# Two edges in the order of ScalarE and VectorE at the start of a gated recurrence

## The chip, the cores and the metric

The kernel runs on one core of one Trainium2 chip. The metric is the time of one execution on the device in microseconds, as the median of several runs; lower is better.

## The reference

One layer of a streaming encoder over 2048 tokens of width 1024, in float32. The input is normalised (RMSNorm) and projected by one matrix to eleven parts, which feed three groups of heads. Group A is a gated linear recurrence with 4 heads of 64x64 state, group B a mixer of trailing-window means, group C an attention with forgetting gates over 8 heads. Each output is gated, the three are concatenated and projected, normalised, and added to the input. The change touches group A:

```python
f_gate = lb + (1.0 - lb) * jax.nn.sigmoid(z)
log_f_a = jnp.log(jnp.maximum(f_gate, TINY))
k_a = (1.0 - lb) * jax.nn.sigmoid(-z)
...
# per chunk, state S: b = cumsum(log_f)
o = attn @ v + (q * exp(b)) @ S        # attn[t, s] = sum_d q[t] k[s] exp(b[t] - b[s]), s <= t
S = exp(b_last)[..., None] * S + (k * exp(b_last - b)).T @ v
```

## The kernel before, in words

The kernel first builds normalised, transposed halves of x (float16 high and low parts, `hTh` and `hTl`), tile by tile of 128 tokens. For each tile `x_parts` runs a square with a row sum on ScalarE (line 213), a scaling on VectorE (214), a power on GpSimd (217), a scaled copy on ScalarE (218), a subtraction on VectorE (220) and two transposing DMAs from SP's queue (221, 223).

The recurrence then goes through eight units `(g, ct)`: four groups of 512 tokens, and in each two halves of 128 channels (two heads). A unit has three parts.

- `hgrn_f` projects the gate input on TensorE (`pf`, 24 matmuls of 512 columns) and makes the features of the unit from it. ScalarE takes `pf` out of its bank (lines 254 and 255); then some twenty instructions of ScalarE, VectorE and GpSimd follow in a chain: `sg` (260), `E`, the running sum `b` (271), `nb` (274), the decayed keys `Kd`, `khat` (286, 287), `Qd`, `qhat` (289), and `el`, the decay of each of the four chunks (291).
- `hgrn_q` projects the queries (`pq`) and multiplies them into `Qd` and `qhat` (lines 301 to 309).
- `hgrn_unit` computes the outputs. Its part up to the first yield forms the nearest-neighbour products `pd` (327), masks them (329), transposes `khat` (`pk`, 333), and copies the result to `khT` on ScalarE (335). Then come six levels (64, 32, 16, 8, 4, 2), two between yields. A level forms differences of `b` on GpSimd (348, 349), their exponential `X` on ScalarE (350), `Z` = X times the queries in two halves on VectorE (355), the product `pl` on TensorE (359) and a masked copy into `at` on VectorE (363). After level 32 the state update takes `pu` = khT times the values (368) and eight updates of `S` on VectorE (378); after level 8 the state's share `po` of the output is formed (383). A last part adds `at` times the values (391), normalises and stores. X has four buffers, Z three.

The loop over the units runs the features of the next unit ahead of the levels of the current one. `fill` puts other projections in between: chunks of attention keys (`kq_chunk`) and token values of group A (`tok_i`). `feed` steps the x tiles from 8 on, one step a level.

The order in which instructions stand in the source isn't the order on an engine. A scheduler of the framework orders each engine's instructions before the program runs, from a cost model, with the order in the source as the priority among those that are ready. On the chip each engine then takes its instructions in that fixed order. `tc.issue_after(ins)` adds an edge to this ordering: every instruction traced in the block that runs on the engine of `ins` comes after `ins` there. It is no semaphore, and instructions of other engines in the block get no edge.

Of the kernel before, what the change touches and what calls it, by code (L numbers as in the profile page):

```python
# [15 lines left out]
AF = mybir.ActivationFunctionType  # L16
ALU = mybir.AluOpType
# [5 lines left out]
P = 128  # L23
# [31 lines left out]
def kernel(  # L55
# [138 lines left out]
            PE.matmul(ps, a[:, k, :], b[:, k, c0:c0 + n], start=i == 0, stop=i == 3 * KC - 1)  # L194


    last_pow = [None]

    xts = {}
    def x_dma(xpool, t, tag="xt"):  # L200
        xt = (xpool if tag == "xt" else ap).tile([P, D], F32, tag=tag, name=f"xt{t}", bufs=2)
        sp(nc.sync.dma_start(xt, xf[t * P:(t + 1) * P, :]))
        xts[t] = xt
# [21 lines left out]
    def x_load(xpool, t, tag="xt"):  # L225
        for _ in x_parts(xpool, t, tag):
            pass
# [20 lines left out]
    def hgrn_f(g, ct, wf, bank=None):  # L248
        u = f"_{g}_{ct}"
        pf = (bank or pj)(f"pf{u}")  # L250
        proj_cm(pf, wf, ct * P, g)
        yield
        z, E = tmp(f"z{u}"), tmp(f"E{u}")
        S.activation(E, pf, AF.Abs, bias=0.0, scale=INV)
        S.activation(z, pf, AF.Copy, bias=0.0, scale=INV)
        S.activation(E, E, AF.Exp, bias=0.0, scale=-1.0)
        S.activation(E, E, AF.Ln, bias=1.0, scale=1.0)
        sg = tmp(f"sg{u}")

        V.scalar_tensor_tensor(sg, z, 0.0, E, op0=ALU.min, op1=ALU.subtract)  # L260
        E1 = V if g == 0 else G
        E1.tensor_tensor(z, sg, z, op=ALU.subtract)
        lk = lbt[:, 8 + ct:9 + ct]

        V.tensor_scalar(E, sg, -43.0, None, op0=ALU.max)
        S.activation(E, E, AF.Exp, bias=0.0, scale=-1.0)
        S.activation(E, E, AF.Ln, bias=lbt[:, 4 + ct:5 + ct], scale=lbt[:, 2 + ct:3 + ct])
        V.tensor_tensor(E, E, sg, op=ALU.add)
        V.tensor_scalar(E, E, lbt[:, 6 + ct:7 + ct], None, op0=ALU.max)
        b = t512("b", f"b{u}")  # L270
        V.tensor_tensor_scan(b, d0, E, initial=0.0, op0=ALU.mult, op1=ALU.add)

        nb = t512("nb", f"nb{u}")
        V.scalar_tensor_tensor(nb, z, lk, b, op0=ALU.add, op1=ALU.subtract)

        lfo = sg
        E1.tensor_tensor(lfo.rearrange("p (n two) -> p n two", two=2),
                        E.rearrange("p (n two) -> p n two", two=2),
                        odd.unsqueeze(1).to_broadcast([P, GT // 2, 2]), op=ALU.mult)
        q_d, k_d = t512("Qd", f"Qd{u}"), t512("Kd", f"Kd{u}")  # L280
        E1.tensor_tensor(k_d, z, lfo, op=ALU.subtract)
        S.activation(k_d, k_d, AF.Exp, bias=lk, scale=1.0)
        S.activation(q_d, lfo, AF.Exp, bias=0.0, scale=1.0)
        kk = t512("khat", f"khat{u}")
        bt = b.rearrange("p (n t) -> p n t", t=P)
        G.tensor_tensor(kk.rearrange("p (n t) -> p n t", t=P), bt[:, :, P - 1:P].to_broadcast([P, 4, P]), nb.rearrange("p (n t) -> p n t", t=P), op=ALU.add)
        S.activation(kk, kk, AF.Exp, bias=0.0, scale=1.0)
        e = t512("qhat", f"qhat{u}")
        S.activation(e, b, AF.Exp, bias=0.0, scale=1.0)
        el = ap.tile([P, 4], F32, tag="el", name=f"el{u}", bufs=2)  # L290
        V.tensor_copy(el, e.rearrange("p (n t) -> p n t", t=P)[:, :, P - 1])
        feats[(g, ct)] = dict(nb=nb, b=b, qd=q_d, kd=k_d, kk=kk, qh=e, el=el)

    def hgrn_q(g, ct, wq):
# [17 lines left out]
    def run(steps):  # L312
        for _ in steps:
            pass

    def hgrn_unit(g, ct, va):
# [15 lines left out]
        for tt in range(4):  # L332
            PE.transpose(pk[:, tt * P:(tt + 1) * P], f["kk"][:, tt * P:(tt + 1) * P], idf)
        khT = t512("khT", f"khT{u}", 1)
        S.activation(khT, pk, AF.Copy, bias=0.0, scale=1.0)
        yield "B"

        for li, h in enumerate(LEVELS):
            X = t512("X", f"X{u}_{h}", 4)
            Z = Zs[zc[0] % NZ]  # L340
            zc[0] += 1
            bv = b.rearrange("p (n two h) -> p n two h", two=2, h=h)
            nbv = nb.rearrange("p (n two h) -> p n two h", two=2, h=h)
            Xv = X.rearrange("p (n two h) -> p n two h", two=2, h=h)
            n = GT // (2 * h)
            mid = bv[:, :, 0, h - 1:h].to_broadcast([P, n, h])
            E1 = G if h in POOL_LV else V
            E1.tensor_tensor(Xv[:, :, 1, :], bv[:, :, 1, :], mid, op=ALU.subtract)
            E1.tensor_tensor(Xv[:, :, 0, :], mid, nbv[:, :, 0, :], op=ALU.add)
            S.activation(X, X, AF.Exp, bias=0.0, scale=1.0)  # L350
            qv = qs.rearrange("p (t n two h) -> p t n two h", t=4, two=2, h=h)
            X5 = X.rearrange("p (t n two h) -> p t n two h", t=4, two=2, h=h)
            for hh in range(2):
                r = slice(64 * hh, 64 * hh + 64)
                V.tensor_tensor(Z[r, :, hh, :].rearrange("p t (n h) -> p t n h", h=h), X5[r, :, :, 1, :], qv[r, :, :, 1, :], op=ALU.mult)
            pl = pm(f"pl{u}_{h}")
            plv = pl.rearrange("p (t u c) -> p t u c", t=4, u=2)
            for tt in range(4):
                PE.matmul(plv[:, tt].rearrange("p u c -> p (u c)"), X[:, tt * P:(tt + 1) * P], Z[:, tt].rearrange("p u c -> p (u c)"),
                          start=tt == 0, stop=tt == 3, skip_group_check=True)  # L360
            n2 = 64 // h
            dst = at.rearrange("p t u (n two h) -> p (t u) n two h", two=2, h=h)[:, :, :, 1, :]
            V.copy_predicated(dst, masks[h].rearrange("p (n h) -> p n h", h=h).unsqueeze(1).to_broadcast([P, 8, n2, h]),
                              pl.rearrange("p (u n h) -> p u n h", u=8, h=h))
            if li == 1:
                pu = pm(f"pu{u}")
                for tt in range(4):
                    PE.matmul(pu[:, tt * P:(tt + 1) * P], khT[:, tt * P:(tt + 1) * P], va[:, tt, ct * P:(ct + 1) * P],
                              start=tt == 0, stop=tt == 3, skip_group_check=True)
                olds = []  # L370
                for tt in range(4):
                    old = Sst[ct][Scur[ct] % NS]
                    Scur[ct] += 1
                    new = Sst[ct][Scur[ct] % NS]
                    olds.append(old)
                    for hh in range(2):
                        r = slice(64 * hh, 64 * hh + 64)
                        V.scalar_tensor_tensor(new[r, r], old[r, r], f["el"][r, tt:tt + 1],
                                               pu[r, tt * P + 64 * hh:tt * P + 64 * hh + 64], op0=ALU.mult, op1=ALU.add)
            if li == 3:  # L380
                po = pm(f"po{u}")
                for tt in range(4):
                    PE.matmul(po[:, tt * P:(tt + 1) * P], f["qh"][:, tt * P:(tt + 1) * P], olds[tt], start=tt == 0, stop=False,
                              skip_group_check=True)
            next(xfeed, None)
            if li % 2 == 1:
                yield "L"
# [200 lines left out]

    run(hgrn_q(0, 0, wq))
    wk0 = load_w([(KCOL, 256)], "k0", pool=gwp)  # L590
    x_load(xpool, 6)
    x_dma(xpool, 8)
    x_load(xpool, 7)
    x_dma(xpool, 9)

    def feed():

# [14 lines left out]
    for n, (g, ct) in enumerate(units):  # L612
        nxt = units[n + 1] if n + 1 < len(units) else None

        def fill(j):
            if n == 0:
                if j % 2 == 0:
                    kq_chunk("k", 0, j // 2, g, wk0, kh_d, kl_d)
            elif n == 1:
                if j < 2:  # L620
                    tok_i(6 + j, wi, toks[1])
            elif ct == 0 and g + 1 < NG:
                t = 4 * (g + 1) + j
                if j == 0:
                    toks[g + 1] = new_tokens(g + 1)
                tok_i(t, wi, toks[g + 1])
            elif ct == 1:
                if j % 2 == 0:
                    kq_chunk("k", 0, j // 2, g, wk0, kh_d, kl_d)
            else:  # L630
                next(kq)
# [5 lines left out]
        if n == 0:  # L637
            fs, qs = hgrn_f(0, 1, wf, pm), hgrn_q(0, 1, wq)
            next(fs)
            next(qs)  # L640
            toks[1] = new_tokens(1)
            tok_i(4, wi, toks[1])
            tok_i(5, wi, toks[1])
            next(gen)
            next(gen)
            run(fs)
            run(qs)
            fill(0)
            next(gen)
            fill(1)  # L650
            fill(2)
            fill(3)
            next(gen)
            prev = gen
            continue
# [547 lines left out]
```

## Time and profile before

| | us |
|---|---|
| median of 3 runs | 1251.47 |
| lowest, highest | 1248.06, 1253.38 |
| the profiled execution | 1248.18 |
| its span, first to last instruction | 1246.4 |
| TensorE busy in the span | 1170.5 |
| VectorE busy | 812.2 |
| ScalarE busy | 609.5 |
| GpSimd busy | 403.7 |

In the profile PE is TensorE, PEld its weight loads, DVE VectorE, ACT ScalarE, POOL GpSimd and SPq the queue of SyncE that issues DMAs. Times in the rows are microseconds from the start of the span, and L with a number is a line of the kernel before. A row of a timeline gives start, time, engine, line, operation, output and inputs, shapes, count, and in brackets the idle time before it with what ended it. The eight units start, by their first product `pd`, at 60.38 us (0,0), 104.25 (0,1), 141.31 (1,0), 174.75 (1,1), 206.74 (2,0) and so on.

### The profile page before, as it was taken

Reading aid. Unit: us, or ns where it says so; the run is one execution under the profiler, and the core shown is the slowest. Engines: PE = TensorE matmul, PEld = TensorE weight load, DVE = VectorE, ACT = ScalarE, POOL = GpSimd, SP = SyncE. Lnnn points to the kernel's source line nnn. Section 1 sums busy time; section 2 is a strip of 40 time slices with the busy share of each in tenths; the row PEclk is TensorE's granted clock in tenths of the full one; section 3 lists DMA queues with packets and bytes.
Section 4 is the critical chain, followed back from the end, with each engine's and each line's share of the span. In section 5 each row is a group of like instructions: output and inputs, shape, how many; then the busy total and the mean of one; then the engine's idle time right before and its main releaser. Section 6 shows DMA issues by size and latency. Waiting matters only on the chain.

```text
span 1246.4 us, 25487 instructions
## 1 busy us (share of the span) xinstructions
PE 1170.5 (94%) x9949; PEld 749.9 (60%) x9949; DVE 812.2 (65%) x1736; ACT 609.5 (49%) x1176; POOL 403.7 (32%) x500
## 2 busy tenths in 40 slices
PE   5877999999999999999999999999989899999998
PEld 3445667655644588884447767755555555555544
DVE  5787878887433243214364799788788888888522
ACT  5756444553121222212122677667767676777611
POOL 2645555553130020002230223234334343434400
PEclk9988999999999999999999999999999999999999
DMA  9646100113175232101112343285223222321263
GB/s 226 184 115 170 44 17 18 52 35 93 43 183 142 71 107 71 35 2 43 26 51 70 89 140 110 69 178 127 67 64 85 68 78 79 65 51 38 80 162 104
DMA packets 168137, 107.56 MB, mean 86 GB/s; under 512 B 95824, under 2 KB 159568, under 8 KB 168016
## 3 DMA queue, kind: packets, MB, share of 16 engines
q1 hardware_dynamic: 166976, 105.92, 32.2%
q8 instruction: 78, 1.28, 0.4%
q14 instruction: 43, 0.35, 0.1%
q10 hardware_dynamic: 1040, 0.00, 0.0%
HBM read 59.62 MB, written 31.59 MB: 73 GB/s over the span
## 4 chain that ended last, share of the span: by engine, by line
PE 62%; DVE 19%; ACT 6%; issue 5%; POOL 4%; DMA 4%; SPq 0%; POOLq 0%; DVEq 0%; ACTq 0%
PE y L1078 11%; PE pq L183 7%; PE pv L194 6%; PE pgc L194 5%; PE pu L183 3%; PE st L1009 3%; PE st L1010 3%; PE pgb L183 3%; PE pk L183 3%; DVE pl L1024 3%; PE mx L973 3%; DVE M L979 3%; PE o L1034 2%; PE o L1035 2%; PE pf L183 2%
## 5 line engine op out<-in xcount | busy, mean ns | idle before, releaser
L1019 ACT ACTIVATE pf<-st,biasg 128x512 f32<-128x512 f32 (+1 forms) x320 | 199.6, 625 | 93.9 <-PE st L1010 53.2
L194 PEld LDWEIGHTS <-hTh 128*128 128x128 f16 x1536 | 151.0, 99 | 44.3 <-DMA hTh<-xh 16.1
L1024 DVE TENSOR_TENSOR pl<-pf,ph 128x512 f16<-128x512 f32 (+1 forms) x213 | 139.9, 658 | 42.4 <-POOL ph L1021 24.8
L1024 POOL TENSOR_TENSOR pl<-pf,ph 128x512 f16<-128x512 f32 (+2 forms) x107 | 114.2, 1067 | 147.7 <-ACT ph L1023 137.6
L979 DVE TENSOR_REDUCE M<-mx 128x1 f32<-128x512 f32 x192 | 129.2, 682 | 9.4 <-PE mx L973 8.5
L1023 ACT ACTIVATE ph<-st,biasg 128x512 f16<-128x512 f32 (+2 forms) x213 | 131.4, 617 | 2.1 <-PE o L1036 2.1
L1034 PE MATMUL o<-Vt,ph 128*128 128x65 f16 x1088 | 129.7, 193 | 2.8 <-DVE oc L1048 2.4
L1035 PE MATMUL o<-Vt,ph 128*128 128x64 f16 x1088 | 130.2, 195 | 0.0
L1036 PE MATMUL o<-Vt,pl 128*128 128x65 f16 x1088 | 129.2, 192 | 0.0
L1021 POOL TENSOR_SCALAR ph<-pf 128x512 f16<-128x512 f32 (+1 forms) x107 | 66.0, 617 | 192.4 <-ACT pf L1019 130.8
L1034 PEld LDWEIGHTS <-ph 128*128 128x128 f16 x1088 | 102.6, 96 | 34.5 <-issue 5.5
L1009 PE MATMUL st<-QQ,K 128*128 128x512 f16 (+1 forms) x320 | 111.5, 349 | 5.6 <-ACT ph L1023 5.0
L1035 PEld LDWEIGHTS <-ph 128*128 128x128 f16 x1088 | 101.8, 97 | 24.5 <-issue 1.1
L1036 PEld LDWEIGHTS <-pl 128*128 128x128 f16 x1088 | 102.3, 99 | 0.4
L1078 PE MATMUL y<-woh,mh 128*128 128x512 f16 (+2 forms) x264 | 98.2, 373 | 0.0
L1078 PE MATMUL y<-woh,ml 128*128 128x512 f16 (+2 forms) x264 | 98.0, 373 | 0.0
L1078 PE MATMUL y<-wol,mh 128*128 128x512 f16 (+2 forms) x264 | 98.0, 373 | 0.0
L973 PE MATMUL mx<-KA,QM 68*128 68x512 f16 (+1 forms) x224 | 79.5, 358 | 5.7 <-DVE M L979 4.1
L194 PEld LDWEIGHTS <-hTl 128*128 128x128 f16 x768 | 75.5, 98 | 9.9
L1010 PE MATMUL st<-QB,KA 68*128 68x512 f16 x224 | 80.1, 358 | 0.0
L1078 PEld LDWEIGHTS <-mh 128*128 128x128 f16 x528 | 49.4, 98 | 50.4 <-issue 0.7
L976 DVE CUSTOM_DVE_ANT_0 mx<-mx,negq 128x128 f32<-128x128 f32 (+3 forms) x128 | 62.3, 492 | 12.0 <-PE mx L973 11.5
(327 smaller groups left out, 2691.1 us busy)
## 6 DMA issues: line engine op xcount, KB each, us to landing
xt<-in_x_dram SPq DMA_DIRECT2D x16, 512.0 KB, 4.4
xr<-in_x_dram SPq DMA_DIRECT2D x16, 512.0 KB, 4.5
out_dram<-yt SPq DMA_DIRECT2D x15, 512.0 KB, 3.1
QQ<-qh_d SPq DMA_DIRECT2D x64, 64.0 KB, 2.3
wo<-in_w_out_dram SPq DMA_DIRECT2D x16, 256.0 KB, 3.0
gc_d<-gtc SPq DMA_DIRECT2D x32, 128.0 KB, 2.0
gtl<-gc_d SPq DMA_DIRECT2D x16, 256.0 KB, 2.9
wst_q<-in_w_in_dram SPq DMA_DIRECT2D x12, 256.0 KB, 2.9
```

The source lines that it names most:

```text
L183: PE.matmul(ps, a[:, k, c0:c0 + P], b[:, k, :], start=i == 0, stop=i == 3 * KC - 1)
L194: PE.matmul(ps, a[:, k, :], b[:, k, c0:c0 + n], start=i == 0, stop=i == 3 * KC - 1)
L979: V.tensor_reduce(dst, mx[:, :w], op=ALU.max, axis=AX.X)
L1009: PE.matmul(st[:, off:], K2[c][:, h, jj * P:(jj + 1) * P], QQs[i][:, off:], start=True, stop=False)
L1010: PE.matmul(st[:, off:], KA[c][:68, h, jj * P:(jj + 1) * P], QBs[i][:68, off:], start=False, stop=not diag)
L1019: S.activation(pf[:, off:], st[:, off:], AF.Exp, bias=bias, scale=0.125)
L1023: S.activation(ph[:, off:], st[:, off:], AF.Exp, bias=bias, scale=0.125)
L1024: (G if k == 1 else V).tensor_tensor(pl[:, off:], pf[:, off:], ph[:, off:], op=ALU.subtract)
L1034: PE.matmul(pov[:, qi, :], ph[:, qs], Vt[:, j, h, 0:65], start=(j == 0 and qi == 0), stop=False, skip_group_check=True)
L1035: PE.matmul(pov[:, qi, 0:64], ph[:, qs], Vt[:, j, h, 65:129], start=False, stop=False, skip_group_check=True)
L1036: PE.matmul(pov[:, qi, :], pl[:, qs], Vt[:, j, h, 0:65], start=False, stop=(j == 4 * g + qi), skip_group_check=True)
L1078: PE.matmul(py, a[:, k, :], b[:, k, cs], start=i == 0, stop=i == 3 * KC - 1)
```

## The change

There are four edits.

1. In `hgrn_f` the first yield moves behind the two instructions that take `pf` out of its bank. This matters only where the steps of `hgrn_f` are run apart, which the first two units do.
2. In the first unit the work after the key copy is put into a block that is ordered behind `khT` on ScalarE: x tiles 6 and 7 (which were loaded ahead of the unit), the loads of tiles 8 and 9, the first two levels of (0,0), and the rest of the features and queries of (0,1). The loads of tiles 6 and 7 alone stay ahead of the unit.
3. The second unit gets an order of its own: the two projections of (1,0) come first, then the unit's own first four levels with their fills, and then the rest of the features and queries of (1,0), ordered on VectorE behind the last Z of the fourth level (level 8).
4. `el` is computed by ScalarE as the exponential of the last column of each chunk of `b`, in place of a copy on VectorE from `qhat` before the query is multiplied in. This is in all eight units.

```diff
@@ hgrn_f
         proj_cm(pf, wf, ct * P, g)
-        yield
         z, E = tmp(f"z{u}"), tmp(f"E{u}")
         S.activation(E, pf, AF.Abs, bias=0.0, scale=INV)
         S.activation(z, pf, AF.Copy, bias=0.0, scale=INV)
+        yield
...
         el = ap.tile([P, 4], F32, tag="el", name=f"el{u}", bufs=2)
-        V.tensor_copy(el, e.rearrange("p (n t) -> p n t", t=P)[:, :, P - 1])
+        S.activation(el, bt[:, :, P - 1], AF.Exp, bias=0.0, scale=1.0)
@@ hgrn_unit
-        S.activation(khT, pk, AF.Copy, bias=0.0, scale=1.0)
+        last_khT[0] = S.activation(khT, pk, AF.Copy, bias=0.0, scale=1.0)
...
-                V.tensor_tensor(Z[r, :, hh, :]..., op=ALU.mult)
+                last_Z[0] = V.tensor_tensor(Z[r, :, hh, :]..., op=ALU.mult)
@@ ahead of the units
-    x_load(xpool, 6)
-    x_dma(xpool, 8)
-    x_load(xpool, 7)
-    x_dma(xpool, 9)
+    x_dma(xpool, 6)
+    x_dma(xpool, 7)
@@ the loop over the units, n == 0
             next(gen)
-            next(gen)
-            run(fs)
-            run(qs)
+            with tc.issue_after(last_khT[0].ins):
+                x_load(xpool, 6)
+                x_dma(xpool, 8)
+                x_load(xpool, 7)
+                x_dma(xpool, 9)
+                next(gen)
+                run(fs)
+                run(qs)
             fill(0)
             next(gen)
             fill(1)
             fill(2)
+            fill(3)
+            next(gen)
+            prev = gen
+            continue
+        if n == 1:
+            fs, qs = hgrn_f(nxt[0], nxt[1], wf), hgrn_q(nxt[0], nxt[1], wq)
+            next(fs)
+            next(prev)
+            next(qs)
+            next(gen)
+            fill(0)
+            fill(1)
+            next(gen)
+            fill(2)
+            next(gen)
+            with tc.issue_after(last_Z[0].ins):
+                run(fs)
+                run(qs)
             fill(3)
             next(gen)
             prev = gen
```

## Rows read from the trace of the kernel before

**Rows 1.** Busy time by stretch: PE, weight loads, DVE, ACT, POOL, PE clock, DMA.

```profile
66.00:76.00 10.00, 4.69 (x15) 2.86 (x16) 6.87 (x12) 8.49 (x15) 5.83 (x6) 0.55 0.38 64
...
86.00:96.00 10.00, 8.66 (x56) 6.04 (x57) 9.75 (x18) 4.08 (x6) 6.35 (x9) 1.00 0.43 103
...
200.00:250.00 50.00, 50.00 (x361) 35.64 (x361) 40.62 (x66) 26.37 (x53) 28.89 (x27) 1.00 0.14 38
```

**Rows 2.** Waits of TensorE, 40 to 126 us: total, times, longest.

```profile
PE pl L359 <- DVE Z L355: 9.6, 2, 7.8
...
PE pu L368 <- ACT khT L335: 6.6, 1, 6.6
```

**Rows 3.** Timeline of TensorE, 61 to 127 us.

```profile
61.47 0.66 PE L333 MATMUL pk<-idf,khat 128*128 128x128 f32 x4
...
71.31 2.08 PE L368 MATMUL pu<-va,khT 128*128 128x128 f32 x8 [6.55 <-ACT khT L335]
...
73.17 3.62 PE L183 MATMUL pk<-hTh,wh_k 128*128 128x512 f16 x8
...
78.63 1.89 PE L183 MATMUL pk<-hTl,wh_k 128*128 128x512 f16 x8
...
87.34 1.13 PE L359 MATMUL pl<-Z,X 128*128 128x128 f32 x8 [1.83 <-DVE Z L355]
...
113.91 1.06 PE L359 MATMUL pl<-Z,X 128*128 128x128 f32 x8
...
122.75 2.05 PE L359 MATMUL pl<-Z,X 128*128 128x128 f32 x8 [7.78 <-DVE Z L355]
...
124.59 1.92 PE L383 MATMUL po<-S,qhat 128*128 128x128 f32 x8
...
126.29 2.94 PE L183 MATMUL pf<-hTh,wh_f 128*128 128x512 f16 x8
```

**Rows 4.** Timeline of ScalarE, 57 to 71 us.

```profile
57.05 0.63 ACT L350 ACTIVATE X<-X 128x512 f32<-128x512 f32 x1
...
66.17 0.63 ACT L266 ACTIVATE E<-E 128x512 f32<-128x512 f32 x1 [3.58 <-DVE E L265]
...
70.67 0.59 ACT L335 ACTIVATE khT<-pk 128x512 f32<-128x512 f32 x1
```

**Rows 5.** Timeline of VectorE, 59 to 121 us.

```profile
59.05 1.69 DVE L220 SCALAR_TENSOR_TENSOR xl<-xt,ss,xh 128x1024 f16<-128x1024 f32 x1
...
103.13 0.69 DVE L260 SCALAR_TENSOR_TENSOR sg<-z,E 128x512 f32<-128x512 f32 x1 [0.87 <-ACT E L257]
...
120.40 0.82 DVE L355 TENSOR_TENSOR Z<-X,qs 64x256 f32<-64x256 f32 x1
```

**Rows 6.** Busy time by stretch, first and second unit, columns as in rows 1.

```profile
60.38:104.25 43.87, 34.88 (x198) 21.33 (x197) 35.74 (x62) 25.68 (x45) 18.92 (x21) 0.88 0.55 138
...
104.25:141.31 37.06, 29.28 (x197) 21.76 (x196) 28.10 (x50) 21.52 (x38) 22.05 (x24) 0.86 0.47 114
```

**Rows 7.** Timeline of GpSimd, the query product of unit (1,0).

```profile
117.40 1.27 POOL L308 TENSOR_TENSOR Qd<-Qd,qs 128x512 f32<-128x512 f32 x1 [0.21 <-DVE qs L307]
```

**Rows 8.** Groups of instructions by form: busy and mean ns, then idle before.

```profile
L291 DVE COPY el<-qhat 128x4 f32<-128x4 f32 x8 | 4.3, 532 | 1.1 <-ACT qhat L289 1.1
...
L240 ACT ACTIVATE fcs<-pi 128x8 f32<-128x8 f32 x12 | 2.1, 177 | 0.0
```

**Rows 9.** Waits of VectorE, both stretches of rows 6: total, times, longest.

```profile
DVE xl L220 <- ACT xh L218: 5.2, 4, 1.8
...
DVE ss L214 <- ACT xh L213: 4.2, 4, 1.9
...
DVE ma L400 <- POOL rs L398: 1.8, 1, 1.8
...
DVE sg L260 <- ACT E L257: 1.7, 2, 0.9
```

**Rows 10.** Waits of TensorE, 126 to 400 us.

```profile
PE pu L368 <- ACT khT L335: 1.5, 1, 1.5
```

More of the change, by code (lines that the diff above doesn't have):

```diff
@@ L194, in proj_tm @@
             PE.matmul(ps, a[:, k, :], b[:, k, c0:c0 + n], start=i == 0, stop=i == 3 * KC - 1)
-    last_pow = [None]
+    last_pow, last_khT, last_Z = [None], [None], [None]
     xts = {}
@@ L354, in hgrn_unit @@
                 r = slice(64 * hh, 64 * hh + 64)
-                V.tensor_tensor(Z[r, :, hh, :].rearrange("p t (n h) -> p t n h", h=h), X5[r, :, :, 1, :], qv[r, :, :, 1, :], op=ALU.mult)
+                last_Z[0] = V.tensor_tensor(Z[r, :, hh, :].rearrange("p t (n h) -> p t n h", h=h), X5[r, :, :, 1, :], qv[r, :, :, 1, :], op=ALU.mult)
             pl = pm(f"pl{u}_{h}")
```

## The prediction

> **What bounds the kernel now.** I read four views in this order. First the busy time by stretch: TensorE works without a gap at full clock in the middle of the recurrence, 50.00 of 50 us with a granted clock of 1.00 [rows 1], and the reader is to see the contrast with 66 to 76 us, where it is busy for 4.69 of 10 us at a clock of 0.55. From about 126 us on TensorE is the engine that everything waits for, so whatever it loses before that time is carried to the end one for one, and whatever it gets back there shortens the kernel one for one.
>
> Second, TensorE's own waits ahead of 126 us: 9.6 us in two waits for Z (VectorE, line 355), the longest 7.8, and 6.6 us in one wait for khT (ScalarE, line 335) [rows 2]. Third, TensorE's timeline, to see where these stand [rows 3]. In the first unit, (0,0), the transposes pk of the key product end at 61.47 + 0.66 = 62.13 us, and pu, which needs their copy khT, starts at 71.31. In the second unit, (0,1), the product of the third level ends at 114.97, and that of the fourth starts at 122.75, 7.78 us later, for want of its Z. After each gap the same matmuls run slower: eight of 128x128 take 2.08 (pu) and 2.05 us (pl) against 1.06.
>
> Fourth, what the two late instructions stood behind. ScalarE has E of line 266 ahead of khT, and sat idle for 3.58 us before it; khT itself started at 70.67, 8.5 us after its input was there [rows 4]. VectorE started the fourth level's Z at 120.40 us, although its buffer was free by 114 us (three Z buffers, so level four takes that of level one, whose product stands before the row at 113.91): between them lie the features of unit (1,0), which began with sg at 103.13 [rows 3, 5].
>
> **The change part by part.** I measure from one pd to the next, the first product of a unit: 60.38 to 104.25 us (first unit) and 104.25 to 141.31 us (second) [rows 6].
>
> *What TensorE can get back.* Idle: 43.87 - 34.88 = 8.99 us and 37.06 - 29.28 = 7.78 us [rows 6]. Cold matmuls: in the first unit pu 2.08 - 1.06 = 1.02 and the first eight of the key chunk 3.62 - 1.89 = 1.73 (the last eight's time); in the second pl 2.05 - 1.06 = 0.99, po 1.92 - 1.06 = 0.86, pf 2.94 - 1.89 = 1.05 [rows 3]. With 2.75 and 2.90 us these make 11.7 and 10.7 us, together 22.4. The cold part comes back only if the gaps that stay are short; one of 1.83 us at 85.5 us was followed by 1.00 clock in 86 to 96 [rows 1, 3].
>
> *The edge behind khT (first unit).* Behind it in ScalarE's queue now stand: the squares and copies of x tiles 6 and 7, the exponentials X of levels 64 and 32, and the rest of the features and queries of (0,1) from the second E on. What is left ahead of khT is the evacuation of pf (the moved yield: two instructions that run in any case, now earlier), the two token copies and, as nothing holds them, X of levels 16 and 8. I expect khT at 62.2 us, so pu at 62.8. What the edge costs: X of level 64 ran at 57.05 [rows 4] and now can't before 62.7, so the products of the first levels slip by 5.6 us. That is covered, since pu (1.06 us) and the two key chunks, 48 matmuls at 1.89 us for eight [rows 3], 11.3 us, are ready for TensorE then. If that cover is gone, the price is the slip, 5.6 us. Tile 6 loses its early place too: its last VectorE step ran at 59.05 for 1.69 us [rows 5], and 1.33 us of that are now added to the first stretch. Its transposes, and those of tile 7, are still wanted only by pf of (1,0), which now runs past 90 us. On SP's queue the load of tile 7 moves ahead of the block and those of 8 and 9 stay behind the tiles whose buffers they take; tiles 8 to 11 are wanted only for the next group, two units on. All of this costs nothing by itself.
>
> *The edge behind level four's Z (second unit).* The features of (1,0) on VectorE now stand behind that Z, which can start when its buffer is free, at 114 us or before on the old time axis. The wait of 7.78 us goes. What is late next is the features themselves, and with them pd of (1,0). From sg (103.13) to Qd's product with the query on GpSimd (117.40 + 1.27 = 118.67) they took 15.5 us [rows 5, 7]. Starting at 114.9, after the two halves of Z, they end at 130.4, and TensorE, with both terms back, would come to pd at 141.31 - 10.7 = 130.6. It just fits.
>
> *The ends by ScalarE.* The copy el cost VectorE 0.53 us, eight times; ScalarE's nearest row for so few columns is 0.18 us [rows 8]. The bound from above is a whole 512-column exponential, 0.63 us [rows 4]. I take 0.18, since four columns are nearer to eight than to 512. Only the two copies in the two stretches count, 2 x 0.53 = 1.06 us of VectorE; the other six lie in units where TensorE doesn't wait for it.
>
> *What VectorE allows.* It is busy for 35.74 + 28.10 us of the two stretches and idle for 8.13 + 8.96 = 17.1 us [rows 6]. With 1.06 us of copies gone and 1.33 us of tile 6 added, 16.8 us is the most that the two stretches can shrink before VectorE is full; that is less than TensorE's 22.4, so VectorE sets the sum. Of its idle time, the waits for x tiles (5.2 + 4.2 us) and for the power on GpSimd (1.8 us) [rows 9] aren't what the edges aim at. If all of these stay, and the 1.7 us for E of line 257 [rows 9], the gain is 16.8 - 9.4 - 1.8 - 1.7 = 3.9 us. If none stays it is 16.8, and the 1.5 us that pu of the third unit waits [rows 10] could go too: 18.3. I take the middle of 3.9 and 16.8, 10.3 us, because some of the x waits, the longest of 1.9 us, stand where ScalarE itself is held up ahead of khT, and because VectorE, once it runs behind the others, reaches such a wait later.
>
> **The sum.** The profiled execution took 1248.18 us, 3.3 us under the median of 1251.47. 1248.18 - 10.3 = 1237.9, and on the scale of the median 1241.
>
> **The rivals.**
> *VectorE is full already.* The gaps on TensorE move instead of closing: VectorE was busy for 9.75 of the 10 us from 86 to 96 [rows 1], and all its waits for other engines but those at the two places stay. Then the gain is 0 to 3.9 us: 1244 to 1248 for the profiled execution, 1248 to 1251 by the median. For it speaks that cap of 16.8 us below TensorE's; against it, that VectorE idled for 17.1 us.
>
> *The wait for the key copy moves to the third and fourth unit (slower).* The features of (1,0) now end only as pd wants them, so those of (1,1) crowd in behind them, and khT of (1,0), which has no edge, falls behind them on ScalarE. The place is pu of units three and four. The price of one such wait is what the first unit paid, 8.5 us from pk's end to khT with 2.75 us of cold matmuls, 11.3 us, less the 1.5 us paid already: 9.8 us. In one unit that cancels the gain of 10.3; in both it gives 1248.18 - 10.3 + 19.6 = 1257.5, 1261 by the median. It decides once the two waits are 10.3 us longer in sum. For it speaks that the wait exists there already; against it, that in these units TensorE lost no more than this 1.5 us [rows 10], as it had the token products of the next group to run meanwhile. The Trainium skill speaks for this rival: "TensorE: Matmul & The Clock Gate", section "Architectural detail", says that the queues of ScalarE and VectorE keep strict order while TensorE may only pull weight loads forward. The trace agrees, since khT stood for 8.5 us behind instructions that it doesn't depend on [rows 3, 4]; so an edge helps the unit in which it is put and nothing else.
>
> *The edges change nothing.* The order on the engines might already put these instructions so. It doesn't: both late instructions stand behind just what the edges hold back [rows 4, 5]. I give it no chance of its own.
>
> **How the numbers follow.** Over 0.5%, 6.3 us, is about what can be told from no change. The forecast (gain 3.9 to 18.3, so 1233 to 1248) gets 0.74, of which 0.66 lies over 6.3 us and 0.08 under; a full VectorE gets 0.15, all within 0.5%; the moved wait gets 0.11, of which 0.08 is slower by over 0.5%. Faster 0.66, same 0.26, slower 0.08. The range from 1232 to 1250 takes in the forecast's bounds and most of the second case and leaves out the slower one.
>
> **What would show it.** Right: khT starts within 1 us of pk's end, near 62 us, and the wait at pu is under 1 us; the granted clock in 66 to 76 us is above 0.9; level four's Z of the second unit stands on VectorE ahead of sg of (1,0), and the wait of 7.8 us is under 3; pd of (1,0) comes near 131 us instead of 141.31; el is on ScalarE at about 0.2 us. Wrong: pk itself comes later than 62 us, so that the whole block behind khT is late; pf of (1,0) waits for the transposes of tiles 6 and 7; pd of (1,0) waits for Qd; or pu of the third and fourth units waits for khT by several us.

## The result, and the profile after

The change makes the kernel slower: 1256.17 us median against 1249.4 us for the kernel before on the same chip, ratio 1.0049 with a 95% interval of 1.0033 to 1.0065. The prediction, 1241 with a range of 1232 to 1250, has the wrong sign. The profiled execution took 1254.89 us (span 1253.2), that of before 1248.18 (span 1246.4).

As before, a unit is measured from its first product `pd` to that of the next; the table in the next section has all seven. (In the kernel before the fifth unit starts at 206.67 us; the 206.74 given ahead of the prediction is wrong.) On the profiled executions the difference adds up: the first `pd` starts 1.12 us later (61.50 against 60.38; in the kernels of this study it lies anywhere from 60.38 to 61.67), the first unit is 3.75 us shorter, the second 1.42 shorter, the third 7.72 longer, units four to six together 3.60 longer, the seventh 0.22 shorter. That makes +7.05 us at the last `pd`, and the spans differ by 6.8. So there are three things to explain: a gain half as large as forecast, a new loss in the third unit, and a loss in three units that no edge touches.

Busy time by stretch in the kernel after: 66 to 76 us, then the first, second and third unit (columns as in [rows 1]).

```profile
61.50:101.62 40.12, 32.65 (x197) 19.77 (x196) 33.70 (x61) 27.50 (x49) 18.05 (x21) 1.00 0.52 128
101.62:137.26 35.64, 28.98 (x198) 20.32 (x197) 21.36 (x38) 17.11 (x31) 18.36 (x21) 0.95 0.52 119
137.26:178.42 41.16, 34.04 (x246) 25.54 (x245) 30.87 (x53) 20.90 (x41) 25.51 (x25) 0.92 0.14 33
66.00:76.00 10.00, 9.52 (x60) 6.11 (x58) 8.03 (x16) 6.44 (x11) 3.82 (x5) 1.00 0.74 155
```

The same view of before, third unit.

```profile
141.31:174.75 33.44, 31.98 (x246) 24.49 (x245) 24.21 (x43) 15.40 (x31) 20.17 (x21) 1.00 0.03 9
```

The cold stretch of the first unit is gone: 9.52 us busy at a clock of 1.00 where before had 4.69 at 0.55 [rows 1]. But look at VectorE (third busy column). In the second unit its work falls from 28.10 us [rows 6] to 21.36, in the third it rises from 24.21 to 30.87: the edge carried 6.7 us of it across `pd`. VectorE was to be the bound; instead its idle time in the first two units grew, from 17.1 us to 6.42 + 14.28 = 20.7.

Waits of TensorE after, 40 to 126 us, and then, below the second "...", 126 to 400 us (total, times, longest).

```profile
PE pl L359 <- DVE Z L355: 8.1, 5, 3.5
PE pf L183 <- DVE k000l L413: 1.8, 1, 1.8
PE pl L359 <- ACT th L304: 1.5, 1, 1.5
PE po L391 <- DVE at L363: 1.0, 1, 1.0
...
PE pi L194 <- ACT fcs L240: 7.1, 1, 7.1
PE pl L359 <- DVE Z L355: 5.3, 3, 1.8
PE po L391 <- DVE at L363: 1.7, 1, 1.7
```

The wait of 6.6 us for khT [rows 2] is gone. The wait of 7.8 us for level four's Z is 3.5. Smaller ones for Z, the key chunk and `at` stand in their place, and there is one of 7.1 us which before doesn't have at all: `pi`, the token products of the third unit, wait for a bank that ScalarE (lines 239 and 240) has to empty. Where it comes from is read on the timelines. First TensorE after.

```profile
62.59 0.66 PE L333 MATMUL pk<-idf,khat 128*128 128x128 f32 x4
...
72.28 1.06 PE L368 MATMUL pu<-va,khT 128*128 128x128 f32 x8
...
115.84 1.13 PE L359 MATMUL pl<-Z,X 128*128 128x128 f32 x8 [3.50 <-DVE Z L355]
...
137.26 1.16 PE L327 MATMUL pd<-Qd,Kd 64*128 64x128 f32 x16
...
154.32 0.38 PE L194 MATMUL pi<-wh_i,hTh 128*128 128x264 f16 x1 [7.12 <-ACT fcs L240]
154.49 0.43 PE L194 MATMUL pi<-wl_i,hTh 128*128 128x264 f16 x1
154.71 0.43 PE L194 MATMUL pi<-wh_i,hTl 128*128 128x264 f16 x1
```

VectorE after, from the fourth level's Z on.

```profile
114.78 0.91 DVE L355 TENSOR_TENSOR Z<-X,qs 64x256 f32<-64x256 f32 x1
115.72 2.47 DVE L378 SCALAR_TENSOR_TENSOR S<-S,el,pu 64x64 f32<-64x64 f32 x8
...
118.83 0.68 DVE L260 SCALAR_TENSOR_TENSOR sg<-z,E 128x512 f32<-128x512 f32 x1
...
137.06 1.88 DVE L355 TENSOR_TENSOR Z<-X,qs 64x256 f32<-64x256 f32 x2 [6.99 <-ACT X L350]
138.97 0.69 DVE L260 SCALAR_TENSOR_TENSOR sg<-z,E 128x512 f32<-128x512 f32 x1
```

GpSimd after, the end of the features of (1,0).

```profile
129.33 1.82 POOL L308 TENSOR_TENSOR Qd<-Qd,qs 128x512 f32<-128x512 f32 x1
131.10 2.44 POOL L348 TENSOR_TENSOR X<-b 128x256 f32<-128x256 f32 x4
133.49 1.05 POOL L286 TENSOR_TENSOR khat<-b,nb 128x512 f32<-128x512 f32 x1
```

ScalarE after, 63 to 154 us.

```profile
63.29 0.60 ACT L335 ACTIVATE khT<-pk 128x512 f32<-128x512 f32 x1 [1.18 <-PE pk L333]
...
134.58 0.63 ACT L287 ACTIVATE khat<-khat 128x512 f32<-128x512 f32 x1 [3.36 <-POOL khat L286]
135.11 0.61 ACT L256 ACTIVATE E<-E 128x512 f32<-128x512 f32 x1
...
153.20 0.63 ACT L287 ACTIVATE khat<-khat 128x512 f32<-128x512 f32 x1 [0.89 <-POOL khat L286]
...
153.84 0.36 ACT L239 ACTIVATE va<-pi 128x256 f32<-128x256 f32 x1
```

And two rows of the kernel before: `sg` of (1,1) on VectorE and the first copy of `pi` in the third unit on ScalarE.

```profile
139.48 0.69 DVE L260 SCALAR_TENSOR_TENSOR sg<-z,E 128x512 f32<-128x512 f32 x1 [0.86 <-ACT E L257]
...
151.55 0.38 ACT L239 ACTIVATE va<-pi 128x256 f32<-128x256 f32 x1
```

The features of (1,0) start with `sg` at 118.83 instead of 103.13 [rows 5], 15.7 us later. Their last parts crowd on GpSimd, where four halves of X for the levels of (1,0) itself (2.44 us) stand ahead of `khat`. ScalarE waits 3.36 us for that `khat`, and behind it in its fixed order stands the second E of the next unit's features, (1,1). VectorE stands still for 6.99 us, until X comes from ScalarE; `sg` of (1,1) follows at 138.97, 1.7 us after `pd` of (1,0). In the kernel before it was at 139.48, 1.8 us ahead of its `pd`. So the features of (1,1) run 3.5 us late against their unit, beside VectorE work that the edge pushed into it, and the copies of `pi` that stand behind their `khat` on ScalarE come at 153.84, 16.6 us after `pd`; in before, 10.2 us after (151.55 - 141.31). TensorE runs out of banks. Behind the gap some twenty `pi` matmuls start 0.22 us apart (154.49, 154.71), ahead of it 0.11: the granted clock of the unit is 0.92, and its busy time 34.04 us against the 31.98 of before, 2.06 more. The sum for the third unit is 7.12 + 2.06, less the 1.46 us (33.44 - 31.98) that before lost there at `pu` [rows 10]: the 7.72 us measured.

### The profile page after: what moved, and what is told of

The parts are those of the page before. It is cut to its first block, busy times and chain, and to the rows that moved or that the text cites. A ratio compares the mean times of both kernels' runs of the same rounds, so it can differ in the third digit from the quotient of the medians.

```text
span 1253.2 us, 25486 instructions
## 1 busy us (share of the span) xinstructions
PE 1171.7 (93%) x9949; PEld 748.8 (60%) x9949; DVE 807.9 (64%) x1728; ACT 608.9 (49%) x1184; POOL 404.4 (32%) x500
## 4 chain that ended last, share of the span: by engine, by line
PE 63%; DVE 20%; issue 4%; ACT 4%; DMA 4%; POOL 3%; SPq 1%; POOLq 0%; DVEq 0%; ACTq 0%
PE y L1101 11%; PE pq L183 8%; PE pv L194 6%; PE pgc L194 6%; PE pk L183 4%; PE st L1032 3%; PE pu L183 3%; PE st L1033 3%; PE pgb L183 3%; PE mx L996 3%; DVE pl L1047 3%; DVE M L1002 3%; PE o L1057 2%; PE o L1058 2%; PE o L1059 2%
```

## The experiments

Four theories were set against each other in the first runs. A: the level-four edge makes the features of (1,0), and behind them those of (1,1), late, and the third unit pays. In its narrow form only the copies of `pi` stand in the wrong place on ScalarE; in the wide form the features themselves are late. B: the edge behind khT costs. C: `el` on ScalarE costs. D: not the edge but the new order in the source (levels ahead of features) costs. All lengths in us, each from one `pd` to the next on the timeline of TensorE. One execution of each kernel was traced, so a length also holds the clock that this execution was granted. With the edge behind khT TensorE's idle time in the first unit is 6.9 to 8.3 us in all nine kernels, but the granted clock is 1.00 in after, e1, h2 and h3, 0.92 in f1, f2, f4 and g3, and 0.88 in e4: hence 40.1 to 44.2 us for the same source up to the place of `el`.

| kernel | ratio to before, 95% interval | unit 1 | 2 | 3 | sum 1-3 | sum 4-6 | 7 |
|---|---|---|---|---|---|---|---|
| before | | 43.87 | 37.06 | 33.44 | 114.37 | 95.56 | 43.97 |
| after | 1.0049 (1.0033-1.0065) | 40.12 | 35.64 | 41.16 | 116.92 | 99.16 | 43.75 |
| e1_unit0 | 0.9996 (0.9984-1.0007) | 40.87 | 35.90 | 36.15 | 112.92 | 95.57 | 43.94 |
| e2_unit1 | 1.0062 (1.0044-1.0079) | 43.37 | 39.04 | 41.00 | 123.41 | 95.54 | 43.95 |
| e3_el | 1.0016 (1.0003-1.0029) | 43.98 | 36.44 | 33.51 | 113.93 | 99.17 | 43.73 |
| e4_both_edges | 1.0038 (1.0023-1.0054) | 44.19 | 32.54 | 40.87 | 117.60 | 95.55 | 43.97 |
| f1_no_edge | 1.0011 (0.9994-1.0027) | 42.41 | 34.83 | 37.85 | 115.09 | 95.55 | 43.87 |
| f2_level2 | 1.0028 (1.0016-1.0040) | 42.34 | 35.53 | 37.97 | 115.84 | 95.54 | 45.77 |
| f4_tok_first | 1.0032 (1.0020-1.0045) | 42.45 | 35.13 | 41.24 | 118.82 | 95.60 | 43.97 |
| g3_levels_first | 0.9992 (0.9976-1.0007) | 42.48 | 35.53 | 33.33 | 111.34 | 95.56 | 43.94 |
| h1_el_late | 0.9994 (0.9983-1.0006) | 43.02 | 37.61 | 33.53 | 114.16 | 95.55 | 43.90 |
| h2_after_el_late | 1.0021 (1.0009-1.0033) | 40.07 | 37.96 | 38.87 | 116.90 | 95.56 | 45.67 |
| h3_g3_el_late | 0.9978 (0.9965-0.9991) | 40.14 | 35.00 | 35.07 | 110.21 | 95.56 | 45.60 |
| g4_before_levels_first | 1.0024 (1.0011-1.0036) | 43.90 | 40.11 | 31.71 | 115.72 | 95.54 | 45.79 |

**e1_unit0.** The edge behind khT and the moved yield alone; the branch `n == 1` is taken out and `el` stays on VectorE.

```diff
-        if n == 1:
-            ...                      # the second unit's own order
-        S.activation(el, bt[:, :, P - 1], AF.Exp, bias=0.0, scale=1.0)
+        V.tensor_copy(el, e.rearrange("p (n t) -> p n t", t=P)[:, :, P - 1])
```

> The edge behind khT with the moved yield alone; the second unit's order and el are those of before. Theory A (the edge behind level four's Z delays the features of (1,0) and, through them, those of (1,1), and TensorE pays in the third unit): the first unit stays 3 to 4 us shorter, the third unit takes 33 to 35 us as before, with no wait of TensorE at pi over 2 us there, and the kernel is 2 to 4 us faster than before. Theory B (the edge behind khT is what costs, as the first levels, tile 6 and the features of (0,1) come late): the 7 us wait in the third unit is there and the kernel is 4 to 7 us slower than before. Theory C (el on ScalarE costs): about 3 us faster, as in A.

The first unit gains 3.0 us and the second 1.2; the third gives 2.7 back, with a wait of 2.1 us for khT and a granted clock of 0.95. The rest, 1.5 us, is too little for the runs to tell from nothing. B falls as a cause of the whole kernel's loss. A's forecast misses too: the third unit was to take 33 to 35 us and the kernel to be 2 to 4 us faster, so the edge isn't shown to pay for itself.

**e2_unit1.** The second unit's order and its edge alone: the block of the first unit and the loads ahead of it are as in before.

```diff
-            with tc.issue_after(last_khT[0].ins):
-                x_load(xpool, 6)
-                ...
+            next(gen)
+            run(fs)
+            run(qs)
```

> The second unit's order with the edge behind level four's Z alone; the first unit and el are those of before. Theory A: the second unit is 1 to 4 us shorter, the third 6 to 8 us longer with TensorE waiting at pi for token copies on ScalarE, and the kernel is 4 to 8 us slower than before. Theory B: no wait of that kind, and the kernel is 1 to 4 us faster. Theory C: as B.

The worst of all: units one to three take 123.41 us, 9.0 more than before, 7.6 of it in the third. This is theory A's part, without the other edge's gain to set against it. The wait at `pi` is 3.1 us here; 3.6 us of the 7.6 are clock (busy time 35.53 against 31.98 us). The second unit, forecast 1 to 4 us shorter, is 2.0 longer: the edge doesn't close the gap that it is aimed at. The waits of TensorE in this kernel's second unit, 104.15 to 143.19 us, begin with

```profile
PE pl L359 <- DVE Z L355: 8.8, 1, 8.8
```

where before had 7.8.

**e3_el.** `el` by ScalarE alone, in all eight units.

```diff
-        V.tensor_copy(el, e.rearrange("p (n t) -> p n t", t=P)[:, :, P - 1])
+        S.activation(el, bt[:, :, P - 1], AF.Exp, bias=0.0, scale=1.0)
```

> el by ScalarE alone, all orders as before. Theories A and B: within 1 us of before. Theory C: 3 to 6 us slower, with longer units from the third on.

The first three units don't show it, but units four to six take 33.32, 32.01 and 33.84 us, to 0.01 the lengths that they have in the whole change, and 3.6 more in sum than before. The ratio alone, 1.0016 (0.4 to 3.6 us), would hardly have found it.

**e4_both_edges.** The whole change with `el` on VectorE.

```diff
-        S.activation(el, bt[:, :, P - 1], AF.Exp, bias=0.0, scale=1.0)
+        V.tensor_copy(el, e.rearrange("p (n t) -> p n t", t=P)[:, :, P - 1])
```

> Both edges without el on ScalarE. Theories A and B: within 1.5 us of the changed kernel, so 5 to 8 us slower than before, with the wait of some 7 us at pi in the third unit. Theory C: within 2 us of before, and no such wait.

Units four to six are back at 95.55; the third unit stays at 40.87, with the wait for `pi` in it (waits of TensorE in this kernel, 137.37 to 178.24 us):

```profile
PE pi L194 <- ACT fcs L240: 6.8, 1, 6.8
```

So the loss has two separate parts: the edges' in the third unit, and that of `el` in units four to six.

**f1_no_edge.** As e4, with the second unit's order in the source kept and only its edge removed.

```diff
-            with tc.issue_after(last_Z[0].ins):
-                run(fs)
-                run(qs)
+            run(fs)
+            run(qs)
```

> Both edges' kernel without el on ScalarE, with the second unit's own order in the source kept but its edge taken away, so that the features of (1,0) go where the scheduler puts them (ahead of level four's Z on VectorE again). Theory A (late features of (1,0) delay those of (1,1), which hold up the third unit): the third unit falls from 40.9 us to 34 to 37, the second takes 35 to 37 again, and the kernel is within 0.2% of before. Rival D (the order in the source, levels ahead of features, is what costs, edge or no edge): the third unit stays at 40 us or more.

The third unit falls from 40.87 to 37.85; without the order in the source as well (e1) it is 36.15. So of the 4.7 us between e1 and e4 the edge makes 3.0 and the order in the source 1.7, and e1 itself was 2.7 over before. By TensorE's idle time in this unit, 2.3, 4.1 and 6.8 us in e1, f1 and e4, the shares are 2.7 and 1.8. Neither forecast of the third unit is met (34 to 37 us, 40 or more): A has the largest of three shares, D has one. The start of `sg` of (1,1) tells the edge's part: with the features of (1,0) behind level four it lies between 0.2 us ahead of `pd` of (1,0) and 3.2 us behind it (after, e2, e4, h2), in all kernels without that edge 0.5 to 4.5 us ahead.

**f2_level2.** As e4, with the features of (1,0) behind the Z of the second level (32) instead of the fourth.

```diff
             next(gen)
+            with tc.issue_after(last_Z[0].ins):
+                run(fs)
+                run(qs)
             fill(2)
             next(gen)
-            with tc.issue_after(last_Z[0].ins):
-                run(fs)
-                run(qs)
```

> The same with the edge kept but tied to the second level's Z (level 32) in place of the fourth's, which is free some 15 us earlier. Theory A: as in f1, the third unit takes 34 to 37 us and the second about 36, since the features start as early as before. Rival D: the third unit stays at 40 us or more.

Held back by two levels less, the third unit takes 37.97 us, as without an edge (A had 34 to 37), with a wait of 3.9 us for khT, and the wait for Z in the second unit is back at 6.6 us. The wait in the second unit and that in the third trade against each other.

**f4_tok_first.** As e4, and in the third unit the features of (1,1) are ordered on ScalarE behind the second pair of `pi`'s copies.

```diff
+        if n == 2:
+            ...
+            fill(0)
+            fill(1)
+            with tc.issue_after(last_tok[0].ins):
+                run(fs)
+                run(qs)
```

> Both edges, el on VectorE, and in the third unit the features of (1,1) ordered on ScalarE behind the unit's first two token copies. Theory A in its narrow form (TensorE waits only for the copies that empty pi's two banks, as these stand behind the features on ScalarE): the wait of 7 us at pi is under 1.5 us, the third unit takes 34 to 36 us, and the kernel is 1 to 4 us faster than before. Theory A in its wide form (the features of (1,1) themselves are late and gate what follows, wherever the copies stand): the wait at pi goes, but pd of (1,1) or the levels then wait, units three and four together stay 5 us or more over the 65.4 of before, and the kernel is no faster than before.

The wait for `pi` is gone and nothing is won, 41.24 us: in its place stands (waits of TensorE in this kernel, 138.36 to 179.60 us)

```profile
PE pl L359 <- DVE Z L355: 6.4, 1, 6.4
```

That is what the wide form forecast: units three and four take 73.2 us, 7.9 over before. But the run doesn't separate the two forms cleanly, since its edge also holds the features of (1,1) back: `sg` starts 12.2 us after `pd`, in e4 1.4 us. It shows that bringing the copies forward at this price wins nothing; a run that moves the copies and leaves the features where they are wasn't made.

**g3_levels_first.** As e1, and in the second unit the first two levels stand ahead of the two token products in the source, with no edge.

```diff
-        fill(0)
-        fill(1)
-        next(gen)
+        if n == 1:
+            next(gen)
+            fill(0)
+            fill(1)
+        else:
+            fill(0)
+            fill(1)
+            next(gen)
```

> The edge behind khT alone, and in the second unit no edge: only the two token projections are moved in the source behind the first two levels, so that TensorE frees the Z buffer of level one 5.4 us sooner. Theory A: the features of (1,0) stay early and level four's Z comes earlier too, so the wait for Z in the second unit falls from 7 to under 3 us without a wait in the third, and the kernel is 3 to 6 us faster than before. Rival D: the gap moves to the third unit again and the kernel is no faster.

The wait for Z in the second unit falls to 1.9 us, as A had it, but 3.6 us of waiting for khT come in there. The third unit is 33.33 us, so levels may be brought forward without its loss if the features aren't pushed back for it. Units one to three together are 3.0 us shorter than before on the traced execution. The kernel was forecast 3 to 6 us faster; by the ratio it can't be told from before, nor from e1.

**h1_el_late.** The kernel before with `el` by ScalarE, ordered behind the query's last exponential. The same edit is in h2 and h3.

```diff
-        S.activation(th, th, AF.Exp, bias=0.0, scale=-1.0)
+        last_th = S.activation(th, th, AF.Exp, bias=0.0, scale=-1.0)
...
+        with tc.issue_after(last_th.ins):
+            S.activation(f["el"], ...[:, :, P - 1], AF.Exp, bias=0.0, scale=1.0)
```

> The kernel before with el by ScalarE in all eight units, as in the run of that edit alone, but ordered behind the last exponential of the query's th (line 305). Everything else is as before. Theory of the place: in units four and six the 0.19 us of el stood ahead of khat and th on ScalarE, the framework then put khT between the two halves of th, qs came 0.9 us later, the power of GpSimd's X with it, and a level's product waited for its Z. With el behind th the lengths of units four to six go back from 33.32, 32.01, 33.84 to 31.9, 31.7, 31.9 us and the ratio is within 0.9985 to 1.0010. Theory of the instruction: the operation costs wherever it stands; the three units stay at 33.3, 32.0, 33.8 and the ratio is 1.0010 to 1.0025.

Units four to six are back at 95.55 us, so the place costs and the instruction doesn't. ScalarE in the fourth unit, before:

```profile
180.40 0.62 ACT L304 ACTIVATE th<-th 128x512 f32<-128x512 f32 x1
181.44 0.63 ACT L287 ACTIVATE khat<-khat 128x512 f32<-128x512 f32 x1 [0.43 <-POOL khat L286]
181.98 0.61 ACT L305 ACTIVATE th<-th 128x512 f32<-128x512 f32 x1
182.50 0.58 ACT L335 ACTIVATE khT<-pk 128x512 f32<-128x512 f32 x1
```

The same in e3:

```profile
180.31 0.19 ACT L291 ACTIVATE el<-b 128x4 f32<-128x4 f32 x1
181.35 0.63 ACT L287 ACTIVATE khat<-khat 128x512 f32<-128x512 f32 x1 [0.85 <-POOL khat L286]
181.89 0.61 ACT L304 ACTIVATE th<-th 128x512 f32<-128x512 f32 x1
182.41 0.58 ACT L335 ACTIVATE khT<-pk 128x512 f32<-128x512 f32 x1
182.88 0.62 ACT L305 ACTIVATE th<-th 128x512 f32<-128x512 f32 x1
```

And in h1:

```profile
182.19 0.61 ACT L303 ACTIVATE th<-th 128x512 f32<-128x512 f32 x1
182.72 0.19 ACT L311 ACTIVATE el<-b 128x4 f32<-128x4 f32 x1
182.81 0.58 ACT L336 ACTIVATE khT<-pk 128x512 f32<-128x512 f32 x1
```

In e3 the 0.19 us of `el` take the slot that the first `th` had while ScalarE waited for `khat`; in the engine's order khT then stands between the two. The last `th` comes 0.90 us later, `qs` on VectorE at 183.54 instead of 182.62, and Qd, qhat and X on GpSimd behind it. VectorE in the fourth unit shows `qs`, before and then e3:

```profile
182.62 0.69 DVE L307 TENSOR_TENSOR qs<-th,pq 128x512 f32<-128x512 f32 x1 [0.60 <-ACT th L305]
```

```profile
183.54 0.69 DVE L307 TENSOR_TENSOR qs<-th,pq 128x512 f32<-128x512 f32 x1 [2.15 <-ACT th L305]
```

Ten microseconds on, TensorE is short of work: 9.58 us busy of 190 to 200 us in before, 8.19 in e3.

```profile
190.00:200.00 10.00, 9.58 (x64) 6.67 (x63) 8.73 (x14) 2.82 (x6) 5.36 (x8) 1.00 0.08 29
```

```profile
190.00:200.00 10.00, 8.19 (x55) 5.77 (x55) 8.93 (x15) 3.59 (x6) 5.18 (x8) 1.00 0.09 29
```

The difference, 1.39 us, is the 1.40 us by which this unit grew.

**h2_after_el_late.** The whole change with `el` behind `th`.

> The whole change, with el behind the query's th as in the run beside it. Theory of the place: units four to six go back to 31.9, 31.7, 31.9 us, so the span falls by about 3 us from the changed kernel's 1253.2 to 1250, ratio 1.0025 to 1.0045; the third unit stays near 41 us, since that is the cost of the edge on VectorE. Theory of the instruction: no change, ratio 1.004 to 1.006.

Units four to six are as before, 95.56 us, and the ratio falls from 1.0049 to 1.0021. That is 3.5 us, as the theory of the place has it, somewhat below the ratios that it gave. The span doesn't show it, 1253.0 us, since the seventh unit of this profiled execution is 1.9 us longer (below). The third unit is 38.87 us instead of about 41 and the second 37.96 instead of 35.64; with the first they make 116.90 us, as in the whole change (116.92): the edges' loss.

**h3_g3_el_late.** g3 with `el` behind `th`.

> The version with the edge behind khT in the first unit and the first four levels ahead of the token products in the second, with el by ScalarE behind th. If VectorE sets the early units, its 0.5 us for each of the eight copies comes back there: units one to three, 42.48 + 35.53 + 33.33 = 111.34 us with the copy on VectorE, come to 109 to 111, and the ratio to 0.996 to 0.999. If el's place on VectorE is free, the three stay at 111.3 and the ratio at 0.9985 to 1.0.

0.9978, 0.9965 to 0.9991: faster than both kernels, by 2.7 us than before. Units one to three come to 110.21 us, 1.1 under g3 and inside the forecast, though its third unit is 1.7 us longer than that of g3. That it is faster than g3 isn't shown, since their intervals overlap; nor that VectorE's copies came back as time, since the first unit's 2.3 us are clock (1.00 against 0.92; its idle time is 7.5 us against 7.0).

**g4_before_levels_first.** The edit of g3 on the kernel before, without the edge behind khT.

> The kernel before, with one thing changed: in the second unit the first two levels stand ahead of the two token products (fill 0 and fill 1) in the source. No edge, el on VectorE. If the order of the second unit alone brought the gain of the version with both, the first unit stays at 43.9 us, the second falls from 37.06 to about 35.5, the third stays at 33.4, and the span is 1.5 us under that of before, ratio 0.998 to 0.9995. If the edge of the first unit is needed for it, the second unit stays at 36.5 to 37.5 us and the ratio at 0.9995 to 1.001.

Both forecasts miss: the second unit is 40.11 us, 3.05 longer than before, and the ratio 1.0024. The third unit gives 1.7 back, so 1.35 us are left over three units, and 1.8 come in the seventh (below). The lines that did no harm behind a shortened first unit don't help behind the old one. The second unit now waits 4.3 us for Z, 2.6 for `ma` (line 400) and 2.0 for khT. Why the order does that wasn't followed further.

## Why the prediction was wrong

**What held.** khT starts at 63.29 us, 0.04 us behind the end of `pk` (62.59 + 0.66), and `pu` comes without a wait. The clock in 66 to 76 us is 1.00. Z of level four stands ahead of `sg`; its wait is less than half of what it was, but 3.50 us and not under 3. `el` takes 0.19 us. Each edge puts its own instruction where it was said to.

**What the first unit got back.** Of its gap of 8.99 us little came back. Its idle time on TensorE falls only to 40.12 - 32.65 = 7.47 us: four waits for Z, 4.6 us, and those for the key chunk and `at`, 1.8 and 1.0, take the place of that for khT. That they come from the slip of the first levels, which was priced at nothing, is argued and wasn't tested. The rest of the 3.75 us is the clock (34.88 - 32.65 = 2.23), and e4, with the same edge, was not granted it (36.97 us busy).

**The step that failed.** It is the level-four edge: "what is late next is the features themselves, and with them pd of (1,0)", "it just fits". The end of the features came as costed: Qd is ready at 129.33 + 1.82 = 131.15 us, forecast 130.4 (`sg` 3.9 us later than forecast, behind the updates of S, and the features 3.2 us shorter). But the account stopped there. The features of (1,1) stand behind those of (1,0) on ScalarE and VectorE, in the same fixed order, and the sum gave the third unit no term. It lost 7.72 us, more than the 3.75 + 1.42 us that the first two gained. e2 (+7.6 us in the third unit with this edge and its order alone) and f1 (3.0 us less without the edge) show that holding these features back costs there. It isn't the only cause: of the 7.4 us that e4 loses in the third unit 2.7 are there with the edge behind khT alone (e1) and 1.7 come with the second unit's order (f1). That the late features act through the copies of `pi` is read from the timelines; f4 doesn't settle it.

**VectorE as the bound.** "VectorE sets the sum" counted its idle time as room to shrink, and took the middle of 3.9 us, where every wait for x tiles stays, and 16.8, where none does. They all stayed: 10.6 us in these two units, against 5.2 + 4.2 [rows 9]. With the features tied behind a late instruction VectorE got more idle time, 20.7 us instead of 17.1, since two waits for X from ScalarE, 8.2 us, came in. So the two units gained 5.17 us, within the bounds and half of the 10.3. `pd` of (1,0) came at 137.26 us, not 131. It waited for no feature then: TensorE had lost 35.64 - 28.98 = 6.66 us in the second unit, to the waits for Z, `th` and `at` that stand above, where 7.78 us had been [rows 6].

**The ends by ScalarE.** "The other six lie in units where TensorE doesn't wait for it" was right about the copy and wrong about what replaced it: 0.19 us in a slot that another instruction needed costs 3.6 us in three units. Half of the whole loss is this term, priced at nothing.

**The rival.** "The wait for the key copy moves to the third and fourth unit" had the cause, features that crowd in behind those of (1,0), and a price of 9.8 us a unit. In the place it missed: the third unit alone pays for them, 7.72 us, and at `pi`, with khT ahead of the crowd and no wait at `pu` there. Its chance of 0.11 was too low, since what spoke against it, that TensorE had token products to run meanwhile, needed ScalarE to empty their banks. The Trainium skill's rule that was set beside it (page "TensorE: Matmul & The Clock Gate", "Architectural detail": strict order in the queues of ScalarE and VectorE) agrees with the traces in both losses: `va` at 153.84 behind `khat`, and `th` behind khT.

## What to carry to other kernels

An edge that holds a chain back moves the whole chain, on every engine that has a part in it, and the next repetition's chain behind it: follow the lateness for one more unit than the one in which the wait is. Read the idle time of an engine as room only if its inputs come no later. An instruction of 0.2 us isn't free on an idle engine whose order is fixed beforehand: it can turn round its neighbours, so compare the engine's order before and after and tie it down where nobody waits.

## What the runs showed of the hardware

The seventh unit comes in two lengths, 43.7 to 44.0 us and 45.6 to 45.8, whatever was changed long before it (f2, h2, h3 and g4 have the longer). TensorE has one gap there in all of them, near 292 us in before and 289 us in h3; it is 1.71 to 1.89 us long in the ten shorter units and 1.91 to 2.01 in the four longer. Busy time by stretch around it, before:

```profile
290.00:295.00 5.00, 3.18 (x26) 2.88 (x25) 4.72 (x14) 1.23 (x2) 1.72 (x3) 1.00 0.37 127
295.00:300.00 5.00, 5.00 (x26) 2.35 (x25) 2.86 (x6) 0.63 (x1) 0.69 (x2) 1.00 0.08 26
```

and h3:

```profile
287.00:292.00 5.00, 3.09 (x24) 2.90 (x23) 4.72 (x14) 1.23 (x2) 1.95 (x4) 0.92 0.36 120
292.00:297.00 5.00, 5.00 (x20) 2.28 (x19) 2.62 (x6) 0.63 (x1) 0.46 (x1) 0.74 0.07 26
```

Busy for 3.18 and 3.09 us of five, one run keeps the granted clock of 1.00 and the other falls to 0.74 in the stretch behind, between the levels of 2.4 and 1.2 GHz, with 20 matmul records instead of 26. By the clock that is 0.08 x 5 + 0.26 x 5 = 1.7 us, and the unit is 1.63 us longer.

The length of a gap alone doesn't decide it. In the first unit e1 and e4 have the same rows on TensorE, 0.04 us apart at most, up to a wait of 2.90 us; e1 goes on at full clock, and in e4 the same eight matmuls behind it take 2.05 us instead of 1.13 (e1, then e4).

```profile
87.19 1.13 PE L359 MATMUL pl<-Z,X 128*128 128x128 f32 x8 [2.90 <-DVE Z L355]
87.15 2.05 PE L359 MATMUL pl<-Z,X 128*128 128x128 f32 x8 [2.90 <-DVE Z L355]
```

With two traces this can't be put down to the one edit between them or to the execution. It is worth 36.97 - 32.58 = 4.39 us of busy time in that unit, as much as most edits here, so two unit lengths of single executions are to be compared by idle time and clock, and not as they stand.
